# In the attention steps of a hybrid layer, all other TensorE work between QK and the product with V, and weight chunks made one ahead

## The chip, the cores and the metric

One core of a Trainium2 chip runs the whole kernel: one layer, 512 tokens, width 1024, all data in fp32. The metric is the device time of one execution in microseconds, lower is better; a kernel's time is the median of several runs. The engines are TensorE (PE; its weight loads are listed as PEld), VectorE (DVE), ScalarE (ACT), GpSimd (POOL) and SyncE (SP), which issues the DMAs here.

## The reference

```python
x = x + 0.5 * swiglu(rms_norm(x), w_gate1, w_up1, w_down1)
u = rms_norm(x) @ w_in          # -> c_q 384 | c_kv 256 | k_rope 32 | MoBA q, k, v 3 x 512
a = mla_attention(...)          # 8 heads, keys of 64 + 32 (rope), V of 64, causal
b = moba_attention(...)         # 8 heads of 64, blocks of 256 keys, top 3 past blocks + own, ALiBi
x = x + concat(a, b) @ w_out
x = x + 0.5 * swiglu(rms_norm(x), w_gate2, w_up2, w_down2)
return rms_norm(x)
```

`mla_attention` makes its queries and its keys and values from the low ranks (`q = rms_norm(c_q) @ w_uq`, `kv = rms_norm(c_kv) @ w_ukv`). With 512 tokens MoBA has two blocks, so every past block is chosen and both groups are causal softmax attention, MoBA's with a bias linear in the distance. The feed-forward width is 2816.

## The kernel before, in words

**Precision.** TensorE takes fp32 operands split in two parts, a high and a low one, and a product is three matmuls: high by high (L326), high by low (L327), low by high (L328), in `mm3`. Whatever feeds a matmul therefore passes ACT, which copies the high part, and DVE (or POOL), which subtracts it to get the low part. For weights these are L251 and L252 in `split`.

**Weights.** They come in chunks by DMA on SP's queue into raw slots. `pump(c, ahead)` makes chunks up to number c + ahead: it splits what has landed, frees the raw slot, and issues the DMA of a later chunk into it (`dma_fill`). The default of `ahead` is 2. For some chunks, those of the V projection, of the four pairs of MLA heads (ap0 to ap3) and of the first half of the output projection (wo0 to wo3), the low part is made by POOL, in two halves of 512 columns. `done(c)` gives the split slots back.

**Attention steps.** There are 16 steps, one per head: eight MoBA heads ("B"), then eight MLA heads ("A"). In step s the loop L1336 to L1344 writes:

- `pt(s-2)`: ten TensorE transposes (L1175) of the normalised scores P of head s-2 into three banks; ACT copies each bank's high part (L1178), DVE its low part (L1179).
- `qk(s)`: QK of head s into three banks (L1112 and L1113 for B, `mm3` for A); DVE adds mask or bias and takes the minimum (L1130, four), then frees the banks; ACT takes exp with row sums (L1138, four).
- `pv(s-2)`: eight matmuls of P by V (L1193) into one bank; ACT copies its lower half out (L1202), DVE adds the upper one (L1204) and frees the bank; each odd head also makes the two parts of the attention output (L1210 on ACT, L1211 on DVE).
- `normalise(s)`: DVE's reciprocal of the row sums (L1143), four multiplications on POOL (L1146), and four DMAs on SP's queue (L1149) that copy P to where `pt` reads it two steps later.
- `fillers(aim)`: pieces of other TensorE work from a queue, taken while half of the next piece still fits under `aim`.

**The fillers** (L1308 to L1325), with the cost in us that the queue writes for each: eight pieces of the MoBA projections of the last four heads, 12 matmuls each, 2.6 (`f_p`; at their end DVE L938, L941 and six half-height copies on ACT, L946, L948 and L949, with the low parts on DVE L947 and L950); four of the V projection, 6 matmuls, 1.3 (`f_uv`); for each pair of MLA heads one key piece, 6 matmuls, 1.3 (`f_uk`; ACT L1260, DVE L1261, and POOL L1262 for the shared rope rows) and two query pieces, 9 matmuls, 1.95 each (`f_uq`; DVE L1273, ACT L1277, DVE L1278); and eight pieces of the output projection's MoBA half, 12 matmuls, 2.6 (`f_wob`; DVE L1295 adds the bank to x). There are eight PSUM banks, handed out in the order in which they come free.

In each step the first call of `fillers` aims at 1.5 + 4.1 s, the second at that plus 3.2, so that some pieces come between QK and the product with V, and some behind `normalise`.

**The order on the engines.** What the program writes is recorded, and a scheduler then sets each engine's order by when it expects operands to be ready. Instructions of neighbouring parts can so change places.

Behind the steps come the remaining parts of the output projection (`wo_part`), which uses the last heads' transposes and products, and then the second feed-forward part, which is most of what follows 572 us.

Of the kernel before, what the change touches and what calls it, by code (L numbers as in the profile page):

```python
# [31 lines left out]
C0 = 128  # L32
OFF = (0, 128, 384, 768)
WARM = 9
LEAD, RATE, BACK = 1.5, 4.1, 3.2
SCRATCH = 1024

_P = 2.0 * math.pi
# [14 lines left out]
def layer_kernel(ctx, tc, xt, xtok, pos_row, pos_tok, gains, fin, consts, w, wc, out):  # L53
# [60 lines left out]
    def balloc():  # L114
        return bfree.popleft()
# [10 lines left out]
    def sput(s):  # L126
        (xfree if s < 8 else sfree if s < NR else efree).append(s)

    def sl(s):
        return ar[:, s, :] if s < NR else ext[s - NR][:, :]  # L130

    def slf(s):
        return sl(s).bitcast(F32)
# [6 lines left out]
    def hi_(s, rows=slice(0, 128)):  # L140
        return sl(s)[rows, 0:512]

    def lo_(s, rows=slice(0, 128)):
        return sl(s)[rows, 512:1024]
# [94 lines left out]
    def dma_fill():  # L239
        while state["dma"] < NCH and (ffree or fextra and state["dma"] in fourth):  # L240
            dma_chunk()
# [13 lines left out]
    def next_step(pieces=1):  # L255
        j = state["step"]
        kind = steps[j][0]
        state["step"] = j + 1
        if kind == "plain":
            c = steps[j][1]  # L260
            p = c in pooled
            hl[j] = split(fl(raw[c]), chunks[c][1], 2 if p else pieces, G if p else None)
            rfree(c)
            return
        if kind in PROD:
            b, q = steps[j][1]
            r = {i: b[i, q] for i in ("11", "12", "22", "21")}

            def add(o, i):
                V.tensor_tensor(fl(raw[r[o]]), fl(raw[r[o]]), fl(raw[r[i]]), op=OP.add)  # L270

            if kind == "q5":
                add("11", "12")
            elif kind == "p6":
                add("11", "22")
                add("12", "22")
            elif kind == "q4":
                add("21", "11")  # L280
                rfree(r["11"])
            i = {"q3": "22", "p7": "12", "p2": "21", "q4": "21"}.get(kind, "11")
            hl[j] = split(fl(raw[r[i]]), 1024)
            if kind in ("q3", "p7", "q4"):
                rfree(r[i])
            return
        _, (q11, q21, q22, q12) = steps[j]
        r = lambda c: fl(raw[c])
        if kind == 0:
            hl[j] = split(r(q11), 1024)  # L290
        elif kind == 1:
            V.tensor_tensor(sq, r(q21), r(q22), op=OP.add)
            hl[j] = split(sq, 1024)
        elif kind == 2:
            V.tensor_tensor(sq, sq, r(q11), op=OP.subtract)  # L295
            hl[j] = split(sq, 1024)
            V.tensor_tensor(r(q21), r(q11), r(q21), op=OP.subtract)  # L297
            rfree(q11)
        elif kind == 3:
            V.tensor_tensor(sq, r(q12), sq, op=OP.subtract)  # L300
            hl[j] = split(sq, 1024)
        else:
            c = (q21, q12, q22)[kind - 4]
            hl[j] = split(r(c), 1024)
            rfree(c)

    def room():
        return len(sfree) + (0 if state["lock"] else len(xfree))

    def pump(c, ahead=2):  # L310
        while state["step"] <= min(c + ahead, NST - 1) and (room() > 1 or state["step"] <= c):
            next_step()
            dma_fill()
# [11 lines left out]
    def mm3(ps, ah, al, bh, bl, start, stop, **kw):  # L325
        T.matmul(ps, lhsT=ah, rhs=bh, start=start, stop=False, **kw)  # L326
        T.matmul(ps, lhsT=ah, rhs=bl, start=False, stop=False, **kw)  # L327
        T.matmul(ps, lhsT=al, rhs=bh, start=False, stop=stop, **kw)  # L328
# [665 lines left out]
    for tp in range(2):  # L994
# [5 lines left out]
        for k in range(8):  # L1000
            c = c_c[k]
# [97 lines left out]
    def qk(s):  # L1099
        g, h = heads[s]  # L1100
        b1, b02, b3 = balloc(), balloc(), balloc()
        where = {0: (b02, 384), 1: (b1, 0), 2: (b02, 0), 3: (b3, 0)}
        for i in ORDER:
            b, o = where[i]
            n = 128 * (i + 1)
            p = banks[b][:, o:o + n]
            ts = slice(i * 128, i * 128 + 128)
            if g == "B":
                c = 512 * (h % 2)
                q = sl(QS["B", h // 2])[:, c + i * 128:c + i * 128 + 128]  # L1110
                kh, kl = KS["B", h // 2]
                T.matmul(p, lhsT=q, rhs=sl(kh)[:, c:c + n], start=True, stop=False)  # L1112
                T.matmul(p, lhsT=q, rhs=sl(kl)[:, c:c + n], start=False, stop=True)  # L1113
            else:
                q, k = QS["A", h], KS["A", h]
                mm3(p, hi_(q)[:, ts], lo_(q)[:, ts], hi_(k)[:, :n], lo_(k)[:, :n], True, True)
        if g == "A":
            sput(QS.pop(("A", h)))
            sput(KS.pop(("A", h)))
        elif h % 2:  # L1120
            sput(QS.pop(("B", h // 2)))
            for k in KS.pop(("B", h // 2)):
                sput(k)
        z = s % 2
        for i in ORDER:
            b, o = where[i]
            n = 128 * (i + 1)
            sc = 2.0 ** -(h + 1) if g == "B" else 1.0
            add = dist[:, OFF[i]:OFF[i] + n] if g == "B" else maskb[:, 512 - n:512]
            V.tensor_tensor_reduce(out=Sc[z][:, OFF[i]:OFF[i] + n], in0=banks[b][:, o:o + n],  # L1130
                                   in1=add, scale=sc, scalar=1e38, op0=OP.add, op1=OP.min,
                                   accum_out=mn[z][:, i:i + 1])
        for b in (b1, b02, b3):
            bfree.append(b)
        for i in ORDER:
            n = 128 * (i + 1)
            p = Sc[z][:, OFF[i]:OFF[i] + n]
            A.activation(p, p, AF.Exp, scale=-1.0, bias=mn[z][:, i:i + 1],  # L1138
                         accum_out=rs[z][:, i:i + 1])

    def normalise(s):
        z = s % 2
        V.reciprocal(ri[z], rs[z])  # L1143
        for i in range(4):
            p = Sc[z][:, OFF[i]:OFF[i] + 128 * (i + 1)]
            G.tensor_scalar(p, p, ri[z][:, i:i + 1], 1.0, op0=OP.mult, op1=OP.mult)  # L1146

            c, o = pcopy(s, i)
            nc.sync.dma_start(slf(c)[:, o:o + 128 * (i + 1)], p)  # L1149
# [4 lines left out]
    def pcopy(s, i):  # L1154
        if i == 1:
            return pq, 512 * (s % 2)
        if s not in PC:
            PC[s] = ealloc()
        return PC[s], {3: 0, 2: 512, 0: 896}[i]
# [3 lines left out]
    def pt(s):  # L1163
        z = s % 2
        PT[s] = {}
        for js in JB:
            b = balloc()
            o = 0
            slot = ealloc()
            for j in js:  # L1170
                PT[s][j] = (slot, o)
                for i in range(j, 4):
                    c, c0 = pcopy(s, i)
                    c0 += j * 128
                    T.transpose(banks[b][:, o:o + 128].bitcast(F32R), in_=sl(c)[:, c0:c0 + 128],  # L1175
                                identity=identr)
                    o += 128
            A.activation(hi_(slot)[:, :o], banks[b][:, :o], AF.Copy)  # L1178
            V.tensor_tensor(lo_(slot)[:, :o], banks[b][:, :o], hi_(slot)[:, :o].bitcast(F32),  # L1179
                            op=OP.subtract)  # L1180
            bfree.append(b)
        sput(PC.pop(s))
# [145 lines left out]
    def fillers(aim):  # L1328
        nonlocal spent
        while pieces and spent + pieces[0][0] / 2 < aim:  # L1330
            cost, c, f, args = pieces.popleft()
            pump(c)
            f(*args)
            spent += cost

    for s in range(16):  # L1336
        if s > 1:
            pt(s - 2)
        qk(s)
        fillers(LEAD + RATE * s)  # L1340
        if s > 1:
            pv(s - 2)
        normalise(s)
        fillers(LEAD + RATE * s + BACK if s < 15 else 1e9)  # L1344


    def wo_part(half, kks, accs, last=False):
# [29 lines left out]
    c = c_wo[6]  # L1377
# [5 lines left out]
    c = c_wo[7]  # L1383
# [163 lines left out]
```

## Time and profile before

| | |
|---|---|
| median of 3 runs | 935.31 us (934.46 to 935.58) |
| the profiled execution | 936.12 us, its span 934.3 us |
| mean granted TensorE clock | 0.998 |
| PE busy | 918.2 us, 98% |
| DVE, ACT, POOL busy | 751.7, 518.0, 138.7 us |
| attention steps | from about 424 to 572 us of the span |

A time in the profile counts from the span's start. A row of the timeline is: start, duration, engine, line, operation, output and inputs, shape, count; in brackets the engine's idle time ahead of it and what ended that. A row of the waits is: engine, output, line, then what released it, with total idle time, count and longest. In a group of instructions the numbers behind the first bar are the busy time and the mean in ns of one, behind the second the idle time before them. Matmuls are pipelined: the duration of one overlaps the next, so consecutive starts tell more than durations.

### The profile page before, as it was taken

The numbers are of one execution on the slowest core, as the hardware profiler recorded it, in microseconds if no ns is written. First come the engines' busy times: TensorE is split into PE (matmuls) and PEld (weight loads), VectorE is DVE, ScalarE is ACT, GpSimd is POOL, SyncE is SP. The second block draws the span as 40 slices with busy tenths as digits, with TensorE's granted clock in tenths as the row PEclk, the third lists the DMA queues.
The fourth block names the chain that finished last, engine by engine and source line by source line (L and its number), as shares of the span: only waits on it lengthen the run. The fifth ranks groups of instructions, "written<-read, shape, count | busy, mean of one in ns | idle before, by whom it ended". The sixth has DMA issues, their size and how long they took to land.

```text
span 934.3 us, 15098 instructions
## 1 busy us (share of the span) xinstructions
PE 918.2 (98%) x5901; PEld 835.8 (89%) x5901; DVE 751.7 (80%) x1091; ACT 518.0 (55%) x832; POOL 138.7 (15%) x172
## 2 busy tenths in 40 slices
PE   8999999999999999999999999999999999999997
PEld 6899999999888888988877788899999999988885
DVE  6999988899988844536789885989798879988845
ACT  7664545457355443627897864755555445735524
POOL 2059401000000000013676530000000000000001
PEclk9999999999999999999999999999999999999999
DMA  9423334236203515233433441123243223711302
GB/s 334 177 90 114 98 120 122 92 113 195 99 5 120 157 38 171 67 131 111 143 127 123 167 147 66 46 90 102 88 129 113 91 90 114 239 54 44 93 0 91
DMA packets 38088, 105.41 MB, mean 113 GB/s; under 512 B 4480, under 2 KB 11264, under 8 KB 38016
## 3 DMA queue, kind: packets, MB, share of 16 engines
q1 hardware_dynamic: 37008, 102.61, 33.6%
q10 hardware_dynamic: 1008, 1.84, 0.5%
q8 instruction: 46, 0.75, 0.3%
q14 instruction: 26, 0.21, 0.1%
HBM read 90.40 MB, written 2.10 MB: 99 GB/s over the span
## 4 chain that ended last, share of the span: by engine, by line
PE 44%; ACT 3%; DVE 2%; issue 2%; POOL 2%; DMA 0%; ACTq 0%; DVEq 0%; POOLq 0%
PE bank L485 22%; PE bank L326 7%; PE bank L327 7%; PE bank L328 7%; PE bank L1193 1%; ACT scr L1138 1%; POOL scr L1146 1%; PE bank L1175 1%; POOL ar L252 0%; ACT ar L251 0%; DVE ext L1179 0%; PE bank L402 0%; DMA ar<-scr 0%; ACT scr L1202 0%; DMA ext<-scr 0%
## 5 line engine op out<-in xcount | busy, mean ns | idle before, releaser
L485 PE MATMUL bank<-ar 128*128 128x256 f32 x3360 | 405.2, 283 | 2.0 <-DVE scr L516 0.8
L485 PEld LDWEIGHTS bank<-ar 128*128 128x128 f32 x3360 | 403.9, 192 | 3.1 <-DVE scr L516 1.3
L251 ACT ACTIVATE ar<-raw 128x1024 fp32r<-128x1024 f32 (+3 forms) x182 | 176.9, 982 | 148.2 <-issue 42.9
L326 PE MATMUL bank<-ar 128*128 128x512 f32 (+4 forms) x664 | 254.6, 384 | 2.5 <-ACT ar L251 1.3
L328 PE MATMUL bank<-ar 128*128 128x512 f32 (+4 forms) x664 | 253.2, 382 | 0.0
L327 PE MATMUL bank<-ar 128*128 128x512 f32 (+4 forms) x664 | 253.0, 381 | 0.1
L252 DVE TENSOR_TENSOR ar<-raw,ar 128x1024 fp32r<-128x1024 f32 (+2 forms) x164 | 192.3, 1182 | 54.3 <-ACT ar L251 35.5
L326 PEld LDWEIGHTS bank<-ar 128*128 128x128 f32 x664 | 124.6, 188 | 25.7 <-ACT ar L251 1.9
L328 PEld LDWEIGHTS bank<-ar 128*128 128x128 f32 x664 | 124.6, 188 | 23.2
L327 PEld LDWEIGHTS bank<-ar 128*128 128x128 f32 x664 | 124.8, 188 | 22.6 <-DVE ar L390 0.5
L251 ACT ACTIVATE ar<-sq 128x1024 fp32r<-128x1024 f32 x62 | 65.7, 1059 | 86.0 <-DVE sq L295 27.0
L252 DVE TENSOR_TENSOR ar<-sq,ar 128x1024 fp32r<-128x1024 f32 x62 | 75.8, 1223 | 10.2 <-ACT ar L251 10.1
L1412 POOL TENSOR_TENSOR x<-x,tabs 128x512 f32<-128x512 f32 x4 | 5.2, 1289 | 353.6 <-ACT scr L354 353.6
L1146 POOL TENSOR_SCALAR scr<-scr,sm 128x128 f32<-128x128 f32 (+1 forms) x64 | 41.2, 664 | 42.4 <-DVE sm L1143 41.6
L617 DVE SCALAR_TENSOR_TENSOR x<-bank,sm,x 128x512 f32<-128x512 f32 x37 | 27.0, 745 | 23.9 <-PE bank L328 23.9
L1138 ACT ACTIVATE scr<-scr,sm 128x256 f32<-128x256 f32 (+1 forms) x64 | 35.3, 553 | 17.9 <-DVE sm L1130 17.9
L495 ACT ACTIVATE scr<-bank 128x512 f32<-128x512 f32 x60 | 34.9, 581 | 6.3 <-PE bank L485 6.3
L354 ACT ACTIVATE scr<-x 128x512 f32<-128x512 f32 x28 | 17.6, 631 | 29.2 <-DVE x L617 27.0
L575 ACT ACTIVATE ar<-h 128x512 fp32r<-128x512 f32 x28 | 17.2, 630 | 17.0 <-PE bank L327 8.8
L252 POOL TENSOR_TENSOR ar<-raw,ar 128x512 fp32r<-128x512 f32 x18 | 23.5, 1320 | 9.2 <-ACT ar L251 8.3
L295 DVE TENSOR_TENSOR sq<-sq,raw 128x1024 f32<-128x1024 f32 x20 | 24.4, 1222 | 0.5
L297 DVE TENSOR_TENSOR raw<-raw,raw 128x1024 f32<-128x1024 f32 x20 | 24.5, 1225 | 0.2
(239 smaller groups left out, 930.2 us busy)
## 6 DMA issues: line engine op xcount, KB each, us to landing
raw<-in_w_dram SPq DMA_DIRECT2D x144, 512.0 KB, 3.5
h<-in_w_dram SPq DMA_DIRECT2D x8, 512.0 KB, 3.8
ext<-scr SPq DMA_DIRECT2D x13, 256.0 KB, 2.4
raw<-in_wc_dram SPq DMA_DIRECT2D x8, 336.0 KB, 3.1
ext<-scr SPq DMA_DIRECT2D x13, 192.0 KB, 2.2
x<-in_xtok_dram SPq DMA_DIRECT2D x4, 512.0 KB, 8.2
ext<-scr SPq DMA_DIRECT2D x16, 128.0 KB, 2.1
xs<-in_xt_dram SPq DMA_DIRECT2D x5, 256.0 KB, 5.2
```

The source lines that it names most:

```text
L251: A.activation(sl(h)[:, a:b], src[:, a:b], AF.Copy)
L252: (e or V).tensor_tensor(sl(l)[:, a:b], src[:, a:b], slf(h)[:, a:b], op=OP.subtract)
L295: V.tensor_tensor(sq, sq, r(q11), op=OP.subtract)
L297: V.tensor_tensor(r(q21), r(q11), r(q21), op=OP.subtract)
L326: T.matmul(ps, lhsT=ah, rhs=bh, start=start, stop=False, **kw)
L327: T.matmul(ps, lhsT=ah, rhs=bl, start=False, stop=False, **kw)
L328: T.matmul(ps, lhsT=al, rhs=bh, start=False, stop=stop, **kw)
L485: T.matmul(o, lhsT=a_[:, ws], rhs=b_[:, xs_], start=first and e == 0 and k == 0 and n == 0, stop=k == 3 and n == 2, skip_group_check=True)
L495: A.activation(t, banks[b], AF.Copy)
L617: V.scalar_tensor_tensor(xs, banks[b], r, xs, op0=OP.mult, op1=OP.add)
L1138: A.activation(p, p, AF.Exp, scale=-1.0, bias=mn[z][:, i:i + 1], accum_out=rs[z][:, i:i + 1])
L1146: G.tensor_scalar(p, p, ri[z][:, i:i + 1], 1.0, op0=OP.mult, op1=OP.mult)
```

## The change

`LEAD` goes from 1.5 to 4.7 and `BACK` (3.2) goes away. 1.5 + 3.2 is 4.7, so a step's aim at its end is what it was. The loop calls `normalise(s)` directly behind `qk(s)`, then all the step's fillers, then the product with V; the last step takes what is left behind it. Within the steps `pump` makes one chunk ahead instead of two.

```diff
-LEAD, RATE, BACK = 1.5, 4.1, 3.2
+LEAD, RATE = 4.7, 4.1
...
-            pump(c)
+            pump(c, 1)
...
         if s > 1:
             pt(s - 2)
         qk(s)
+        normalise(s)
         fillers(LEAD + RATE * s)
         if s > 1:
             pv(s - 2)
-        normalise(s)
-        fillers(LEAD + RATE * s + BACK if s < 15 else 1e9)
+        if s == 15:
+            fillers(1e9)
```

The pieces per step stay the same ones, up to one piece of the last steps. TensorE in step 5, from the end of QK of head 5 to the product of head 3 (L1193), before; the `mm3` into bank4 and bank1 are V-projection pieces:

```order
L1113 MATMUL bank5_86<-ar_61 128x512
L326 MATMUL bank4_85<-ar_61 128x512
L327 MATMUL bank4_85<-ar_61 128x512
L328 MATMUL bank4_85<-ar_61 128x512
L326 MATMUL bank4_85<-ar_61 128x512
L327 MATMUL bank4_85<-ar_61 128x512
L328 MATMUL bank4_85<-ar_61 128x512
L1193 MATMUL bank7_88<-ext5_3129,ext6_3130 128x512 x2
L326 MATMUL bank1_82<-ar_61 128x512
L327 MATMUL bank1_82<-ar_61 128x512
L1193 MATMUL bank7_88<-ar_61,ext7_3131 128x384
```

The same place after, from the last matmul of the first piece on; the transposes (L1175) are already those of head 4, and bank5 is the one that the product of head 2 held:

```order
L328 MATMUL bank4_85<-ar_61 128x512
L1175 MATMUL bank7_88<-identr_76,ext10_3134 128x128
L1175 MATMUL bank7_88<-identr_76,ext1_3125 128x128
L1175 MATMUL bank3_84<-identr_76,ext1_3125 128x128
L326 MATMUL bank5_86<-ar_61 128x512
L327 MATMUL bank5_86<-ar_61 128x512
L328 MATMUL bank5_86<-ar_61 128x512
L326 MATMUL bank5_86<-ar_61 128x512
L327 MATMUL bank5_86<-ar_61 128x512
L328 MATMUL bank5_86<-ar_61 128x512
L326 MATMUL bank1_82<-ar_61 128x512
L327 MATMUL bank1_82<-ar_61 128x512
```

Four more matmuls into bank1 and then the product of head 3 follow. Before, six matmuls stood between QK and the product, now 18 and three transposes.

POOL around the normalisation (L1146) of heads 10 and 11, before; L252 from raw1 is the second chunk of the output projection, wo1, and the L1146 are those of heads 9 and 10:

```order
L1146 TENSOR_SCALAR scr_74<-scr_74,sm_78 128x512
L252 TENSOR_TENSOR ar_61<-raw1_63,ar_61 128x512 x2
L1262 TENSOR_SCALAR ar_61<-ar_61 64x1024
L1262 TENSOR_SCALAR ext3_3127<-ar_61 64x1024
L1146 TENSOR_SCALAR scr_74<-scr_74,sm_78 128x128
L1146 TENSOR_SCALAR scr_74<-scr_74,sm_78 128x256
L1146 TENSOR_SCALAR scr_74<-scr_74,sm_78 128x384
L1146 TENSOR_SCALAR scr_74<-scr_74,sm_78 128x512
```

After, where the first L1146 is the last of head 10 and the next four are those of head 11:

```order
L1146 TENSOR_SCALAR scr_74<-scr_74,sm_78 128x512
L252 TENSOR_TENSOR ar_61<-raw1_63,ar_61 128x512
L1146 TENSOR_SCALAR scr_74<-scr_74,sm_78 128x128
L1146 TENSOR_SCALAR scr_74<-scr_74,sm_78 128x256
L1146 TENSOR_SCALAR scr_74<-scr_74,sm_78 128x384
L1146 TENSOR_SCALAR scr_74<-scr_74,sm_78 128x512
L252 TENSOR_TENSOR ar_61<-raw1_63,ar_61 128x512
```

Both halves of wo1 stood ahead of head 10's normalisation; now the second half stands behind head 11's.

DVE in step 11, behind the last mask instruction (L1130) of head 11, before; L252 is a weight chunk's low part, L1143 the reciprocal:

```order
L1273 SCALAR_TENSOR_TENSOR scr_74<-bank7_88,tabs_73 128x512
L252 TENSOR_TENSOR ar_61<-raw0_62,ar_61 128x1024
L1278 TENSOR_TENSOR ext5_3129<-scr_74,ext5_3129 128x512
L1204 TENSOR_TENSOR scr_74<-bank1_82,scr_74 64x512
L1143 RECIPROCAL sm_78<-sm_78 128x4
L1295 TENSOR_TENSOR x0_69<-bank2_83,x0_69 128x512
L1211 TENSOR_TENSOR ar_61<-scr_74,ar_61 128x512
```

After:

```order
L1273 SCALAR_TENSOR_TENSOR scr_74<-bank5_86,tabs_73 128x512
L252 TENSOR_TENSOR ar_61<-raw5_67,ar_61 128x1024
L1143 RECIPROCAL sm_78<-sm_78 128x4
L1278 TENSOR_TENSOR ext0_3124<-scr_74,ext0_3124 128x512
L252 TENSOR_TENSOR ar_61<-raw0_62,ar_61 128x1024
L1295 TENSOR_TENSOR x0_69<-bank1_82,x0_69 128x512
L1204 TENSOR_TENSOR scr_74<-bank2_83,scr_74 64x512
```

The reciprocal stood behind L1278 and the evacuation of the product (L1204); now it stands ahead of both, and L1204 behind L1295.

## The prediction

> **What bounds the kernel now.** I read the page's busy shares first, then the stretch of the attention steps by itself, then what TensorE waits for in it, then the places one by one in the timeline.
>
> ```profile
> PE 918.2 (98%) x5901; PEld 835.8 (89%) x5901; DVE 751.7 (80%) x1091; ACT 518.0 (55%) x832; POOL 138.7 (15%) x172
> ```
>
> TensorE is busy for 918.2 of 934.3 us. The change neither adds nor removes a matmul, so all that it can give is time in which TensorE stands, and only in the steps that it reorders. Two windows divide these from what follows (start and end, length, then busy time of PE, PEld, DVE, ACT and POOL, then granted clock):
>
> ```profile
> 424.00:572.00 148.00, 144.06 (x814) 121.10 (x813) 120.89 (x283) 114.41 (x267) 75.07 (x94) 1.00 0.40 136
> 572.00:926.00 354.00, 354.00 (x2376) 328.48 (x2375) 289.11 (x348) 180.15 (x242) 5.16 (x4) 1.00 0.27 87
> ```
>
> Behind 572 us TensorE never stands, so what is won ahead of it is won at the end, one for one, and what is lost there too. In the steps it is busy 144.06 of 148.00. DVE (120.89) and ACT (114.41) are not full, so this is a matter of which wait ends when. The waits of PE in that window name their causes (total, count, longest):
>
> ```profile
> PE bank L326 <- DVE ar L1261: 1.4, 2, 1.0
> PE bank L1193 <- ACT ar L1178: 1.0, 1, 1.0
> PE bank L1193 <- DVE ext L1179: 0.8, 3, 0.3
> PE bank L1193 <- DVE ar L1261: 0.4, 1, 0.4
> PEld bank L1175 <- DMA ar<-scr: 0.4, 2, 0.2
> PEld bank L1112 <- DVE scr L1204: 0.4, 1, 0.4
> ```
>
> These understate the loss, since a modelled end of a matmul reaches into the wait that follows. The better measure is start to start, less what the columns take. Columns are priced from the longest run without a wait, the 12 matmuls of one piece of the output projection:
>
> ```profile
> 520.87 0.62 PE L1193 MATMUL bank<-ext,ext 128*128 128x512 f32 x2
> 522.10 0.45 PE L326 MATMUL bank<-ar 128*128 128x512 f32 x1
> 524.89 0.96 PE L1175 MATMUL bank<-identr,ext 128*128 128x128 f32 x10
> ```
>
> From 522.10 to 524.89 are 12 matmuls of 512 columns, 0.233 us each; the eight of a product with V take 522.10 - 520.87 = 1.23 us. By this measure, the product with V that waits longest:
>
> ```profile
> 467.09 0.40 PE L327 MATMUL bank<-ar 128*128 128x512 f32 x1
> 468.51 0.45 PE L1193 MATMUL bank<-ar,ext 128*128 128x384 f32 x1 [1.02 <-ACT ar L1178]
> ```
>
> 468.51 - 467.09 is 1.42, less 0.23: 1.19 lost, and 0.11 behind it. Done for every place of the window that loses over 0.1 us (followers of 0.11 counted with it), the products with V lose 0.61 (at 450.0), 1.30 (468.5), 0.11 (476.4), 0.68 (484.1), 0.27 (502.3), 0.50 (512.2), 0.66 (528.4) and 0.11 (565.5): **4.24**. Two matmuls that wait for a bank lose more, both behind L1261:
>
> ```profile
> 501.56 0.50 PE L326 MATMUL bank<-ar 128*128 128x512 f32 x1 [0.41 <-DVE ar L1261]
> 516.64 0.34 PE L328 MATMUL bank<-ext,ar 128*128 128x384 f32 x1
> 518.01 0.50 PE L326 MATMUL bank<-ext,ar 128*128 128x512 f32 x1 [1.03 <-DVE ar L1261]
> 518.58 0.39 PE L328 MATMUL bank<-ext,ar 128*128 128x512 f32 x1
> ```
>
> The second is 1.37 from 516.64, less 0.17 for 384 columns: 1.20, with its follower 1.31; the first 0.79 by the same count; together **2.10**. The first transposes behind the DMA of P lose **0.63**, a QK that waits for the bank of L1204 **0.38** (the PEld rows above). In all 7.35 us: the change cannot give more than that, and 0.2% of the time, about what a measurement of this kernel can tell from no change, is 1.87.
>
> **The change, part by part.**
>
> *Fillers ahead of V.* Before, steps 3, 7, 9, 12, 13 and 15 had hardly a matmul between QK and the product with V; after, each step has at least 12, that is 12 x 0.233 = 2.8 us more for the transposes' halves (L1178, L1179) to be made. The largest of these waits was 1.30, so I take all eight away: **-4.24**. That holds where the half was late by its own work. The 1.30 was not: ACT had six copies ahead of L1178.
>
> ```profile
> 464.08 1.29 ACT L946 ACTIVATE ext<-scr 64x512 fp32r<-64x512 f32 x2
> 467.35 0.63 ACT L949 ACTIVATE ext<-scr 64x512 fp32r<-64x512 f32 x1
> 467.88 0.84 ACT L1178 ACTIVATE ar<-bank 128x512 fp32r<-128x512 f32 x2
> 463.31 0.73 DVE L938 SCALAR_TENSOR_TENSOR scr<-bank,cst,rB 128x512 f32<-128x512 f32 x1
> ```
>
> *What is late next there.* The copies run from 464.08 to 467.98, 3.9 us. In the new order the whole projection of that step ends just ahead of step 4's V, so what stands behind the copies is no longer L1178 but the evacuation of that product (L1202, L1204), whose bank the second V-projection piece of step 5 takes. Their prices and the work that runs on TensorE meanwhile:
>
> ```profile
> L1204 DVE TENSOR_TENSOR scr<-bank,scr 64x512 f32<-64x512 f32 x16 | 10.9, 684 | 7.2 <-ACT scr L1202 7.2
> L1202 ACT ACTIVATE scr<-bank 64x512 f32<-64x512 f32 x16 | 9.5, 597 | 3.1 <-PE bank L1193 2.8
> 471.73 0.97 PE L1175 MATMUL bank<-identr,ext 128*128 128x128 f32 x10
> 472.54 0.35 PE L1112 MATMUL bank<-ext,ext 128*128 128x256 f32 x1
> 473.88 0.39 PE L326 MATMUL bank<-ar 128*128 128x512 f32 x1
> ```
>
> Chain: 0.73 + 3.9 + 0.60 + 0.68 = 5.9. TensorE: product 1.23, transposes 0.81 (471.73 to 472.54), QK 1.34 (to 473.88), six matmuls 1.40, three early transposes 0.24: 5.0. A new wait of 0.9, or 1.3 if it is as long as the one it replaces; I take **+1.1**.
>
> *Banks behind L1261.* Two such waits stay possible (the query piece of step 8, the third bank of QK 11), at other places. Nothing in the trace shows them in the new order: none at the least, twice 1.31 at the most; I take the middle, 1.3, against 2.10 before: **-0.8**.
>
> *Chunks one ahead.* Before, POOL split the second chunk of the output projection (wo1), both halves, at
>
> ```profile
> 508.73 2.54 POOL L252 TENSOR_TENSOR ar<-raw,ar 128x512 fp32r<-128x512 f32 x2
> ```
>
> and the piece that first uses it began at 522.10, 13 us later. The splits are the same in number; each comes one piece group later, and with it the weight load that takes its raw slot on SP's queue. With such a lead a chunk later is hidden in most places. Not here: wo1 now takes slots that the last query pieces of steps 10 and 11 still read, and POOL's order becomes first half, normalise of head 11, second half. The last two matmuls of step 11's piece (L327, L328) wait for that second half. The rows:
>
> ```profile
> 518.60 0.68 DVE L1278 TENSOR_TENSOR ext<-scr,ext 128x512 fp32r<-128x512 f32 x1
> 521.16 0.68 DVE L1130 CUSTOM_DVE_ANT_0 scr<-bank,cst 128x512 f32<-128x512 f32 x1
> 522.37 1.21 DVE L252 TENSOR_TENSOR ar<-raw,ar 128x1024 fp32r<-128x1024 f32 x1
> 537.79 0.40 PE L328 MATMUL bank<-ar,ext 128*128 128x512 f32 x1
> 538.90 0.69 DVE L1130 CUSTOM_DVE_ANT_0 scr<-bank,cst 128x512 f32<-128x512 f32 x1
> L1273 DVE SCALAR_TENSOR_TENSOR scr<-bank,tabs 128x512 f32<-128x512 f32 x8 | 5.4, 680 | 0.7 <-PE bank L328 0.7
> L1143 DVE RECIPROCAL sm<-sm 128x4 f32<-128x4 f32 x16 | 2.8, 176 | 7.8 <-ACT scr L1138 7.8
> 488.36 3.30 POOL L1146 TENSOR_SCALAR scr<-scr,sm 128x128 f32<-128x128 f32 x4
> 515.20 2.07 POOL L1146 TENSOR_SCALAR scr<-scr,sm 128x128 f32<-128x128 f32 x4 [1.45 <-DVE sm L1143]
> 519.81 1.29 POOL L252 TENSOR_TENSOR ar<-raw,ar 128x512 fp32r<-128x512 f32 x1 [2.54 <-ACT ar L251]
> ```
>
> From the end of a QK to the end of its L1130: 1.57 (538.90 + 0.69 less 537.79 + 0.23) to 3.03 (521.16 + 0.68 less 518.58 + 0.23). Then on DVE L1273 0.68, a split 1.21, the reciprocal 0.18; on POOL the four L1146, 2.07 to 3.30, and the half, 1.29. Sum 7.0 to 9.7. TensorE has meanwhile 18 matmuls (4.2), the product with V, one matmul and three transposes (1.23 + 0.23 + 0.24): 5.9. A new wait of 1.1 to 3.8; middle **+2.5**.
>
> *Normalise ahead of the fillers.* DVE's reciprocal now stands ahead of L1278, L1295 and L1204, and these wait with it for exp's sums. L1204 is wanted only for a bank some pieces on, and P not until two steps later (its four DMAs on SP's queue go out earlier), so nothing. If that cover is gone, it costs what the L1143 row shows, 7.8 / 8 = 1.0 at a place.
>
> *Sum.* Kept 0.63 and 0.38; new 1.1, 1.3, 2.5, and 0.11 behind each of the three, 0.3: 6.2 against 7.35, **-1.2**. The profiled execution took 936.12 us, 1.8 beyond its span, so its own forecast is 934.9; it lies 0.8 above the median of 935.31, and from the median it is **934.1**.
>
> [...]
>
> ```profile
> 510.00 1.82 DVE L1278 TENSOR_TENSOR ext<-scr,ext 128x512 fp32r<-128x512 f32 x1
> ```
>
> L1278 takes 0.68 alone (at 518.60) and 1.82 beside POOL's split of 508.73. [...]
>
> **The rivals.**
>
> R1, the new order covers all: wo1's half is in time (L1130 early as at 538.90, L1146 2.07, and the scheduler finds other matmuls ahead), and L1261's banks are free. Left are 0.63, 0.38, the 1.1 and one bank wait of 0.5: 2.6, that is -4.8: **930.5**. For it: the products of steps 4, 8, 11, 13 and 14 lose nothing even before. Against it: the row of 521.16.
>
> R2, slower, one mechanism: POOL's row at step 11. If the first half of wo1 starts only when the reciprocal is done, it stands in the chain too: 9.7 + 1.3 - 5.9 = 5.1, and with L1261's banks held as long as before (DVE being as late as at 521.16), 0.63 + 0.38 + 1.1 + 2.1 + 5.1 + 0.3 = 9.6, +2.3: **937.6**. The whole is slower than before once that place loses over 7.35 - (0.63 + 0.38 + 1.1 + 2.1 + 0.3) = 2.8 us, and by over 0.2% from 4.7. For it: ACT's L251 came late in before too (POOL waited 2.54 for it at 519.81). Against it: in POOL's new row the first half stands ahead of head 11's L1146.
>
> R3, POOL and DVE stretch each other at step 11: the four L1146 take 3.30, not the middle 2.69, wait 3.1: **934.8**. [...]
>
> R4, the change does less than it says: the scheduler had already drawn matmuls forward (at 467.09 a filler stands just ahead of V), and each wait returns at another place: **935.3**.
>
> **How the numbers follow.** The forecast has 0.45, its own range 932.0 to 936.0 from the ends of the three estimates taken not all at once; 0.13 of that lies more than 0.2% below the median (under 933.4). R1 has 0.23, R2 0.13, R3 0.11, R4 0.08. Faster 0.13 + 0.23 = 0.36; slower 0.13; same the rest, 0.51. The range goes into R1 and up to R2: 930.8 to 937.0 leaves out about 0.1 at either end.
>
> **What would show it.** Right: no wait of over 0.2 us at L1193 in the steps; a wait of about 1 us at a V-projection matmul of step 5 behind L1204; one of 1 to 4 at L327 of step 11 behind POOL's L252; nothing lost behind the steps. Wrong: a V product still behind L1179, the step-11 wait absent (R1) or over 3.8 (R2), or a new wait in a step that I took as covered.

## The result: 1.1% slower, and the profile after

The changed kernel takes 945.29 us (median of 4 runs, 944.19 to 946.66) against 935.14 us before: a ratio of 1.0107, interval 1.0095 to 1.0119. The forecast was 934.1 in a range of 930.8 to 937.0; the rival that was slower stood at 937.6. The time lies beyond both.

The profiled execution took 946.66 us, its span is 944.8. From the first matmul of QK of head 0 to the last of the last product with V, TensorE took 144.8 us before and 154.9 after (10.1 more); behind that it took 356.0 us in both. So the loss lies where it was looked for, in the attention steps, and what follows was not touched. What was not expected is in two lines of the page after, TensorE's busy time and its granted clock in the 40 slices:

```profile
PE 924.1 (98%) x5901; PEld 843.3 (89%) x5901; DVE 753.0 (80%) x1091; ACT 517.1 (55%) x832; POOL 141.2 (15%) x172
PEclk9999999999999999999999799999999999999999
```

The same 5901 matmuls are busy for 5.9 us longer than before (918.2), and one slice has a clock of 7 tenths where before all had 9. Finer windows of after (the clock is the last but two of the columns) show where:

```profile
424.00:582.00 158.00, 148.91 (x814) 127.10 (x813) 121.54 (x282) 113.14 (x267) 77.16 (x94) 0.96 0.37 126
494.64:498.05 3.41, 3.41 (x10) 2.67 (x9) 2.80 (x11) 3.11 (x10) 1.28 (x1) 0.50 0.34 135
521.95:525.36 3.41, 3.41 (x9) 2.67 (x8) 2.44 (x10) 1.89 (x6) 0.92 (x1) 0.50 0.56 204
532.19:539.02 6.83, 6.57 (x24) 5.79 (x25) 5.24 (x14) 3.18 (x9) 0.21 (x1) 0.50 0.51 196
```

TensorE ran at half its clock for three stretches of 3.41, 3.41 and 6.83 us, each beside the end of a wait: the first two begin 1.3 and 0.8 us behind it (494.64 and 521.95, the waits end at 493.35 and 521.15), the third 0.3 us ahead of it (532.19, 532.46). In the timeline of after a matmul of 512 columns then takes 0.43 us from start to start, not 0.23:

```profile
495.01 0.63 PE L326 MATMUL bank<-ar 128*128 128x512 f32 x1
495.44 0.63 PE L327 MATMUL bank<-ar 128*128 128x512 f32 x1
```

Counted matmul by matmul (start to start, less the columns at full clock, in these stretches alone, without the waits in them) that is 1.4 + 1.6 + 2.9 = **5.9 us**. The other 10.1 - 5.9 = **4.2** are waits. The list of PE's waits in the steps, after:

```profile
PE bank L327 <- POOL ar L252: 3.2, 2, 2.9
PE bank L1175 <- DMA ext<-scr: 2.2, 2, 1.2
PE bank L326 <- DVE ext L1261: 1.6, 1, 1.6
PE bank L326 <- DVE ar L1261: 0.9, 1, 0.9
PE bank L326 <- DVE scr L1204: 0.7, 1, 0.7
PE bank L1112 <- DVE scr L1204: 0.3, 1, 0.3
```

No product with V (L1193) waits any more: eight waits of 4.24 us are gone, as the change meant them to be. In their place stand fewer and longer ones. Start to start they are these.

*Step 5, 2.55 us.* The scheduler put three transposes of head 4 ahead of the second V-projection piece, and P of head 4 was not there. PE, POOL, ACT and DVE of after:

```profile
466.24 0.39 PE L328 MATMUL bank<-ar 128*128 128x512 f32 x1
467.61 0.25 PE L1175 MATMUL bank<-identr,ext 128*128 128x128 f32 x1 [0.99 <-DMA ext<-scr]
469.07 0.37 PE L1175 MATMUL bank<-identr,ext 128*128 128x128 f32 x2 [1.20 <-DMA ext<-scr]
463.67 3.97 POOL L1146 TENSOR_SCALAR scr<-scr,sm 128x128 f32<-128x128 f32 x4 [0.94 <-DVE sm L1143]
466.98 0.59 ACT L1202 ACTIVATE scr<-bank 64x512 f32<-64x512 f32 x1
467.81 0.68 DVE L1204 TENSOR_TENSOR scr<-bank,scr 64x512 f32<-64x512 f32 x1
```

Head 4's four multiplications took 3.97 us on POOL, beside DVE's L947 and L950, which read two SBUF tiles each; four such took 2.07 at 515.20 of before, where the DVE instructions beside them (L1261, L1204, L1273) read a PSUM bank and one tile. No run shows whether the DVE instructions beside them made the difference. The bank that the forecast spoke of, of head 2's product, comes free at 468.5 (L1204's end), hidden behind the transposes. The matmul of 466.24 was through its columns at 466.5, so without the transposes that bank alone would have made TensorE wait for 2.0 us: the transposes add 0.5.

*Banks behind the evacuations of key pieces, 2.2 us in step 8 and 1.9 at QK of head 11.*

```profile
490.81 0.40 PE L328 MATMUL bank<-ar 128*128 128x512 f32 x1
491.90 0.51 PE L326 MATMUL bank<-ar 128*128 128x512 f32 x1 [0.69 <-DVE scr L1204]
493.35 0.51 PE L326 MATMUL bank<-ar 128*128 128x512 f32 x1 [0.94 <-DVE ar L1261]
519.21 0.34 PE L328 MATMUL bank<-ar 128*128 128x384 f32 x1
521.15 0.50 PE L326 MATMUL bank<-ar 128*128 128x512 f32 x1 [1.61 <-DVE ext L1261]
517.42 0.57 ACT L1260 ACTIVATE ext<-bank 64x512 fp32r<-64x512 f32 x1
519.56 0.58 ACT L1260 ACTIVATE ext<-bank 64x512 fp32r<-64x512 f32 x1
520.41 0.69 DVE L1261 TENSOR_TENSOR ext<-bank,ext 64x512 fp32r<-64x512 f32 x1
```

ACT copies the first half of a key piece (L1260) behind the step's exp, the second only at 519.56, behind three other copies; DVE's L1261 follows at 520.41, and QK at 521.15. The first of the two waits of step 8 is one behind L1204, the evacuation of a product.

*Second half of wo1 in step 11, 3.1 us.*

```profile
521.73 0.43 PE L328 MATMUL bank<-ar 128*128 128x512 f32 x1
529.13 0.43 PE L1175 MATMUL bank<-identr,ext 128*128 128x128 f32 x3
532.46 0.79 PE L327 MATMUL bank<-ar 128*128 128x512 f32 x1 [2.90 <-POOL ar L252]
525.80 0.69 DVE L1273 SCALAR_TENSOR_TENSOR scr<-bank,tabs 128x512 f32<-128x512 f32 x1 [1.41 <-PE bank L328]
527.54 0.17 DVE L1143 RECIPROCAL sm<-sm 128x4 f32<-128x4 f32 x1
521.59 1.28 POOL L252 TENSOR_TENSOR ar<-raw,ar 128x512 fp32r<-128x512 f32 x1
527.81 3.36 POOL L1146 TENSOR_SCALAR scr<-scr,sm 128x128 f32<-128x128 f32 x4 [4.94 <-DVE sm L1143]
531.15 1.25 POOL L252 TENSOR_TENSOR ar<-raw,ar 128x512 fp32r<-128x512 f32 x1
```

From the reciprocal on this is the chain of the forecast: normalisation of head 11, second half, matmul. Both of its sums came out longer, though. From the end of QK 11 (521.73 + 0.23) to the end of the half (531.15 + 1.25) are 10.4 us, where 7.0 to 9.7 were forecast, because L1273 waited 1.41 for a query piece that TensorE did at half clock; TensorE's own work from there to the transposes at 529.13 took 7.4, not 5.9, for the same reason. The difference, 3.1, fell into the range.

Besides, 0.6 us stay at the first transposes, 0.6 at a QK, and 0.8 are new behind the half of another chunk at 557. Sum 11.8 against 7.35, 4.4 more, which fits the 4.2.

### The profile page after: what moved, and what is told of

It reads as the page before. It is cut to its first block, busy times and chain, and to the rows that moved or that the text cites. A ratio compares the mean times of both kernels' runs of the same rounds, so it can differ in the third digit from the quotient of the medians.

```text
span 944.8 us, 15116 instructions
## 1 busy us (share of the span) xinstructions
PE 924.1 (98%) x5901; PEld 843.3 (89%) x5901; DVE 753.0 (80%) x1091; ACT 517.1 (55%) x832; POOL 141.2 (15%) x172
## 4 chain that ended last, share of the span: by engine, by line
PE 86%; DVE 5%; issue 4%; POOL 3%; ACT 1%; DMA 1%; ACTq 0%; SPq 0%; DVEq 0%; POOLq 0%
PE bank L485 40%; PE bank L327 14%; PE bank L328 14%; PE bank L326 14%; POOL scr L1146 2%; PE bank L1193 1%; POOL ar L252 1%; DVE ar L252 1%; PE bank L1175 1%; PE bank L402 1%; DMA gn<-in_gains_dram 0%; DVE raw L297 0%; POOL xs L727 0%; PE bank L1112 0%; DVE h L469 0%
## 5 line engine op out<-in xcount | busy, mean ns | idle before, releaser
L485 PEld LDWEIGHTS bank<-ar 128*128 128x128 f32 x3360 | 403.8, 192 | 3.2 <-DVE scr L516 1.4
L326 PE MATMUL bank<-ar 128*128 128x512 f32 (+3 forms) x676 | 260.8, 386 | 4.8 <-DVE ext L1261 1.6
L327 PE MATMUL bank<-ar 128*128 128x512 f32 (+3 forms) x676 | 259.8, 385 | 3.2 <-POOL ar L252 3.2
L328 PE MATMUL bank<-ar 128*128 128x512 f32 (+3 forms) x676 | 259.3, 384 | 0.0
L252 DVE TENSOR_TENSOR ar<-raw,ar 128x1024 fp32r<-128x1024 f32 (+2 forms) x164 | 192.9, 1185 | 57.5 <-ACT ar L251 50.8
L326 PEld LDWEIGHTS bank<-ar 128*128 128x128 f32 x676 | 128.4, 190 | 29.4 <-ACT ar L251 2.2
L327 PEld LDWEIGHTS bank<-ar 128*128 128x128 f32 x676 | 128.5, 190 | 27.1 <-POOL ar L252 4.2
L328 PEld LDWEIGHTS bank<-ar 128*128 128x128 f32 x676 | 128.5, 190 | 23.7
L252 DVE TENSOR_TENSOR ar<-sq,ar 128x1024 fp32r<-128x1024 f32 x62 | 75.9, 1224 | 10.2 <-ACT ar L251 10.1
L1146 POOL TENSOR_SCALAR scr<-scr,sm 128x128 f32<-128x128 f32 (+1 forms) x64 | 43.1, 691 | 55.2 <-DVE sm L1143 42.3
L1179 DVE TENSOR_TENSOR ext<-bank,ext 128x512 fp32r<-128x512 f32 (+1 forms) x46 | 25.7, 601 | 0.3
L252 POOL TENSOR_TENSOR ar<-raw,ar 128x512 fp32r<-128x512 f32 x18 | 23.5, 1312 | 8.8 <-ACT ar L251 7.5
```

Of the source, the lines that this page charges most:

```text
L252: (e or V).tensor_tensor(sl(l)[:, a:b], src[:, a:b], slf(h)[:, a:b], op=OP.subtract)
L485: T.matmul(o, lhsT=a_[:, ws], rhs=b_[:, xs_], start=first and e == 0 and k == 0 and n == 0, stop=k == 3 and n == 2, skip_group_check=True)
```

## The experiments

All were compared with runs of the kernel before on the same chip. "Steps" is TensorE's time from the first QK to the last product, of the profiled execution; "half" the time at half clock in it.

| kernel | median us | ratio to before | steps us | half us |
|---|---|---|---|---|
| before | 935.1 to 935.7 | | 144.8 | 0 |
| after | 945.29 | 1.0107 (1.0095 to 1.0119) | 154.9 | 13.7 |
| wo1's low part on DVE | 939.18 | 1.0036 (1.0024 to 1.0049) | 147.5 | 3.4 |
| 12 matmuls in the wait | 943.45 | 1.0084 (1.0070 to 1.0098) | 149.6 | 0 |
| 12 matmuls, no wait | 941.36 | 1.0057 (1.0044 to 1.0071) | 149.9 | 3.4 |
| order alone | 942.11 | 1.0072 (1.0053 to 1.0092) | 149.8 | 6.8 |
| one ahead alone | 940.58 | 1.0051 (1.0036 to 1.0067) | 148.7 | 0 |
| after, normalise behind V | 949.11 | 1.0142 (1.0125 to 1.0160) | 157.6 | 17.1 |
| before, normalise early | 936.47 | 1.0005 (0.9996 to 1.0014) | 144.4 | 0 |
| wo1 and head 4 on DVE | 940.10 | 1.0049 (1.0035 to 1.0063) | 147.6 | 3.4 |
| order in six steps | 936.05 | 1.0006 (0.9997 to 1.0015) | 144.4 | 0 |
| order alone, query first | 940.60 | 1.0055 (1.0041 to 1.0069) | 149.7 | 10.2 |
| before, query first | 936.55 | 1.0005 (0.9996 to 1.0014) | 144.8 | 0 |
| six steps, query first | 942.39 | 1.0062 (1.0049 to 1.0074) | 150.8 | 10.2 |

**Is the half clock set off by the waits?** The first run takes the longest wait away, in the new kernel:

```diff
-    pooled = {steps[j][1] for j in [c_uv, *c_ap, *c_wo[:4]]}
+    pooled = {steps[j][1] for j in [c_uv, *c_ap, c_wo[0], *c_wo[2:4]]}
```

> The new kernel, with the low part of wo1 made by DVE instead of POOL (in one piece of 1024, not two of 512). Theory A: the step-11 wait of 3.1 us goes, and with it the two windows of 3.41 us at half clock that follow it, which cost 3.4: 945.3 - 6.5 = 938.8, range 937.5 to 940.5. If slow windows are not set off by waits: 945.3 - 3.1 = 942.2, with as much time at half clock as before the edit.

Measured 939.18, 6.1 less than after, though only 3.1 of waiting were removed. Its windows show full clock where after had half (530 to 540), and one stretch of half clock, behind step 5, where after had none:

```profile
470.24:473.65 3.41, 3.41 (x10) 2.74 (x10) 2.08 (x5) 2.29 (x8) 0.56 (x1) 0.50 0.08 29
530.00:540.00 10.00, 10.00 (x55) 8.42 (x53) 8.54 (x20) 5.69 (x15) 3.75 (x6) 1.00 0.60 202
```

Not all of the 6.1 comes from the removed wait and its stretch. The waits of step 8 and of QK 11 are still there, nearly as long as in after (0.9 and 1.6), and are no longer followed by half clock (0.99 is the clock of its steps, what the one stretch makes it):

```profile
PE bank L326 <- DVE ext L1261: 1.4, 1, 1.4
PE bank L326 <- DVE ar L1261: 1.0, 1, 1.0
```

In the profiled executions the steps are 7.4 us shorter: 3.1 of waiting, 2.9 of the stretch behind it, and the rest because half clock now follows one of the other waits and not two. So this run alone does not show that the stretch hung on the wait that was removed; the next two bear on it more directly.

The second run leaves the cause of the wait and takes the idling: TensorE gets work in it.

```diff
+            if half == 0 and t == 0 and kk == 3:
+                d = balloc()
+                for _ in range(12):
+                    T.matmul(banks[d], lhsT=hi_(attnT[7])[:, 0:128], rhs=whi(c1)[:, 512:1024],
+                             start=True, stop=True)
+                bfree.append(d)
             wo_mm((c0, c1)[kk // 2], kk % 2, 4 + kk, t, b, kk == 0, kk == 3)
```

> The new kernel with 12 more matmuls (2.8 us of columns), whose results nobody reads, in TensorE's order just ahead of the one that waited 3.1 us for wo1's second half in step 11. They run while it would wait. If the slow windows are set off by TensorE's idling (theory A): the wait shrinks below 0.5 us, the windows of half clock at 532 to 539 go, and 2.8 us more of work make the kernel faster by up to 3.4: 941.5 to 943.5. If slow windows have another cause, or come with the work: 945 (hidden, nothing else moves) to 948.

The control has the same 12 matmuls in the kernel with wo1's low part on DVE, where TensorE does not wait there:

> Control for the run with 12 more matmuls: the same 12 in the kernel with wo1's low part on DVE (939.2), where nothing waits at that place. Theory A: they cost their columns, 12 x 0.233 = 2.8 us: 941 to 943. If 12 more matmuls help TensorE by themselves (as they did where it waited): 939 or less.

With the wait, 12 more matmuls made the kernel 1.8 us faster (943.45 against 945.29); without it, 2.2 slower (941.36 against 939.18). By the ratios to before on the same chip it is 2.2 faster and 2.0 slower, each uncertain by about 1.7. The place in the timeline of the first:

```profile
528.87 0.39 PE L326 MATMUL bank<-ar 128*128 128x512 f32 x1
530.04 0.50 PE L327 MATMUL bank<-ar 128*128 128x512 f32 x1 [0.79 <-POOL ar L252]
```

and the window of its steps, at full clock throughout in this execution:

```profile
424.00:578.00 154.00, 147.01 (x831) 125.54 (x831) 122.44 (x283) 114.00 (x268) 76.62 (x94) 1.00 0.39 130
```

The wait did not shrink below 0.5 as expected, but to 0.9, and the gain is at the lower end of what was expected. With 2.2 us less of waiting and 2.8 more of work, waits alone would have made the kernel 0.6 slower. The profiled execution is the fastest of the four (941.79, mean clock 0.998); the others took 942.69 to 944.37 at 0.994 to 0.996, so they probably had half clock elsewhere, which no trace shows. In the profile the waits of step 5, step 8 and QK 11 were there (2.2, 0.7 + 1.0 and 1.6 us in its list of waits), and no half clock followed, which leads to the next point.

**Which wait sets it off.** Length alone does not tell. In after step 5's 2.55 us were followed by full clock (1.00 from 466 to 490), the 2.2 of step 8 and the 1.9 at QK 11 by half. The starts of its half-clock stretches are 27.31 and 10.24 us apart, 8 and 3 times 3.41. Let its steps be divided into pieces of 3.41 us that begin and end there, and let TensorE stand in the time from start to start that the columns do not take. Then it stood for 2.0 us from 491.23 to 494.64, 2.0 from 518.54 to 521.95 and 2.9 from 528.78 to 532.19, and half clock follows each of the three. The next fullest piece has 1.8 us (467.34 to 470.75; the division parts step 5's 2.55), and full clock follows. Divided in the same way from the half clock at its end (929.93), before has at most 1.3 us in a piece, and a clock of 1.00 in all its steps. In the other runs, too, the same wait went with either clock: the transposes of step 5 waited for 2.2 us by the lists of the kernel with wo1 on DVE and of that with the 12 matmuls, and half clock followed at 470.24 in the first and nowhere in the second. That the place of a wait in such a division decides is the author's reading of the traces of after and before, and so is the 2.0 us in the expectations of two of the last runs, below; neither was shown for the other runs. Why the stretch of after at 532 lasted for 6.83 us, though TensorE stood for only 0.7 us of its first half, is not settled.

**Which part of the change makes the waits.** The order alone, with chunks two ahead and normalise behind the product (the diff is against after):

```diff
-            pump(c, 1)
+            pump(c)
...
         qk(s)
-        normalise(s)
         fillers(LEAD + RATE * s)
         if s > 1:
             pv(s - 2)
+        normalise(s)
```

> The order of the fillers alone: all between QK and the product with V, chunks two ahead as before, normalise behind the product as before. Theory A: no wait for wo1; the waits of step 5's early transposes (2.5 us) and behind L1261 (about 4) stay with one or two slow windows (1.7 each): 936 to 941. Theory B (chunks one ahead are the whole cause): 933 to 936. Theory C (the order is the cause): 944 to 946.

942.11, a little beyond theory A's range. Its profile has 2.2 us more waiting than before (149.8 - 144.8 = 5.0, less 2.8 for 6.8 us at half clock, counted as above). The longest wait reads

```profile
520.20 0.40 PE L326 MATMUL bank<-ar 128*128 128x512 f32 x1
523.27 0.79 PE L326 MATMUL bank<-ext,ar 128*128 128x512 f32 x1 [2.68 <-DVE ext L1261]
```

and step 5's transposes wait for 3.3 us. Behind the wait of the row, matmuls of 512 columns start 0.42 us apart (523.87 to 524.29). The chunks one ahead alone, in the old loop (`pump(c, 1)`, nothing else):

> The old loop (fillers on both sides of the product with V, normalise behind it), with chunks one ahead as the only edit. Theory A (TensorE loses 3.4 us more to waits and 6.8 us to windows at half clock that these waits set off; the waits come from the order of the fillers together with the late second half of wo1): POOL's row has both halves of wo1 between heads 10 and 11 here, so they come late by 1 us at most: 935 to 938 us, no window at half clock in the steps. Theory B (chunks one ahead are the whole cause): 944 to 946. Theory C (the fillers' order alone is the cause): 935.

940.58: theory A's range missed by 2.6 us. Its waits are many and short, 3.8 us more in the steps than before, and the clock stays full there:

```profile
424.00:575.00 151.00, 143.86 (x809) 120.02 (x808) 122.18 (x282) 114.16 (x267) 75.56 (x94) 1.00 0.40 133
```

The longest of its waits in all, by cause:

```profile
PE bank L327 <- POOL ar L252: 1.7, 3, 0.8
PE bank L1112 <- DVE scr L1204: 1.3, 1, 1.3
```

So neither part is the whole cause: alone they cost 7.0 and 5.4 us, and with normalise early, as in after, together 10.1. The order pays more in clock than in waits, the chunks pay in waits alone. Of their 5.4 the steps of the profiled execution show 3.8; it was 1.0 us longer ahead of the steps too, as were executions with chunks two ahead (that of normalise early in the old loop, for one), so this is not put down to the chunks. Normalise's place, in the new loop and in the old:

```diff
         qk(s)
-        normalise(s)
         fillers(LEAD + RATE * s)
         if s > 1:
             pv(s - 2)
+        normalise(s)
```

> The new loop, with normalise put back behind the product with V. Theory A: POOL still has head 11's normalisation between the two halves of wo1, so the step-11 wait stays (2 to 3 us and its slow windows); if the early reciprocal holds up L1261 and L1204 on DVE, the two bank waits go: 939 to 943. If normalise's place in the loop does nothing (the scheduler places it): 944 to 946. Theories B and C both: 944 to 946.

> The kernel before, with normalise written directly behind QK as the only edit. TensorE's order stays that of the kernel before up to a few matmuls in the last step. Theory A (order of the fillers and lateness of the chunks make the waits, normalise's place does not): 935 to 936.5, no window at half clock in the steps. If the early reciprocal holds up DVE: 938 or more.

The first of these two is also the order and the chunks together without the third edit: 14.0 us over before, more than 7.0 + 5.4. Put back behind the product in the new loop, normalise costs 3.8 us more than in after (949.11), which no theory had: QK 11 waits for 4.8 us there,

```profile
526.88 0.79 PE L326 MATMUL bank<-ext,ar 128*128 128x512 f32 x1 [4.59 <-DVE ext L1261]
```

and in the old loop, early, it changes nothing that can be told (936.47 against 935.53). The early reciprocal is not the fault; in the new loop it saves time.

**Can it be mended?** With wo1 on DVE, head 4's multiplications were put there too, so that the scheduler leaves its transposes behind the product:

```diff
-            G.tensor_scalar(p, p, ri[z][:, i:i + 1], 1.0, op0=OP.mult, op1=OP.mult)
+            (V if s == 4 else G).tensor_scalar(p, p, ri[z][:, i:i + 1], 1.0, op0=OP.mult,
+                                               op1=OP.mult)
```

> The new kernel with wo1's low part on DVE (the earlier run, 939.2) and, besides, the four multiplications of head 4's normalise on DVE instead of POOL. The scheduler then leaves head 4's transposes behind the product of step 5. Theory A: the wait of 2.5 us for the DMA of head 4's P in step 5 goes and the slow window behind it (1.7), but a V-projection piece waits about 1.1 us for the bank of head 2's product, as was forecast: 939.2 - 2.5 - 1.7 + 1.1 = 936.1, range 935 to 938. If the wait only moves: 939.

940.10, missed: the transposes no longer wait, but the V-projection piece does, for the bank of head 2's product (L1204 stands one line lower here):

```profile
466.52 0.40 PE L328 MATMUL bank<-ar 128*128 128x512 f32 x1
470.49 0.79 PE L326 MATMUL bank<-ar 128*128 128x512 f32 x1 [3.57 <-DVE scr L1205]
```

It is the wait that the forecast put here, at 3.7 us, not 1.1, since DVE now has the multiplications, and the low parts behind them, ahead of L1205: it starts at 469.75, though ACT's copy was done at 467.9. The other trials move fillers in six steps of the old loop only, or change the order of two pieces (in the order alone, in the kernel before, and in the six steps):

```diff
-        fillers(LEAD + RATE * s)
+        fillers(LEAD + RATE * s + (BACK if s in (3, 7, 9, 12, 13, 15) else 0))
```

> The kernel before, with the fillers moved ahead of the product with V in steps 3, 7, 9, 12, 13 and 15 only, where hardly a matmul stood there; chunks two ahead, normalise behind. Theory A: the products' waits in these steps go (0.6 + 0.7 + 0.3 + 0.7 + 0.1 = 2.4 us), nothing long enough for a slow window comes: 932.7 to 935. If each wait returns elsewhere: 935.1; if one of over 1.8 us comes with a slow window: 937 or more.

```diff
-        pieces.append((1.3, c_ap[j], f_uk, (j,)))
         pieces.append((1.95, c_ap[j], f_uq, (j, 0)))
+        pieces.append((1.3, c_ap[j], f_uk, (j,)))
```

> The order alone with chunks two ahead (the earlier run, 942.1), and in each pair of MLA heads the first query piece ahead of the key piece, whose bank is freed latest (two copies on ACT, then two subtractions on DVE, L1261). Theory A: the wait of 2.85 us of QK 11 behind L1261 goes with its slow window (1.7): 937 to 939. If the bank wait comes from the place ahead of the product with V and not from the kind of piece: 941 to 943.

> The kernel before, with each pair's first query piece ahead of its key piece as the only edit. Theory A: the two bank waits behind L1261 (0.79 and 1.31 us) go or shrink, no window has 2 us of idle TensorE: 933 to 935. If the bank waits move to other pieces: 935.5 to 936.5.

> The fillers ahead of the product with V in six steps, and the first query piece ahead of the key piece. Theory A: as the run of the six steps (936.05), less the bank waits of 0.72 and 1.32 us behind L1261, no slow window: 933.5 to 936. If waits fall together in one window of 3.41 us with 2.0 us or more of idle TensorE, 1.7 is added: 937 to 938.

Six steps: 936.05, no change, missed by 1. Query first: 940.60, missed; the waits behind L1261 shrink, but transposes now wait for a P,

```profile
508.96 0.28 PE L1175 MATMUL bank<-identr,ar 128*128 128x128 f32 x1 [1.65 <-DMA ar<-scr]
```

with half clock behind it (from 510.29 on 384 columns take 0.31 us, not 0.17). Query first in the old order: 936.55, no change, missed by 1.5, with no half clock in the steps. Both: 942.39, missed, 10.2 us at half clock. None of these versions beats the kernel before.

## Why the prediction was wrong

Right: what bounds the kernel; that the products' eight waits go (-4.24); that nothing moves behind the steps; that step 11 would wait for wo1's second half behind head 11's normalisation (forecast 2.5 of 1.1 to 3.8, measured 3.1, with L1146 at 3.36, just over its long end); that normalise's place costs nothing. That the 3.1 lies inside its range is in part luck: the chain took 10.4, beyond its longest, 9.7, and the work that covers it 7.4, not 5.9.

Wrong in size, by its terms:
- *Step 5*, forecast 1.1, measured 2.55. The three early transposes stood in the order rows, and were counted as cover of 0.24 us; that they need head 4's P nearly a step early, behind an L1146 that took 3.97, was not asked. The bank wait lay hidden behind them, and was itself larger, 2.0 where 1.1 was forecast: the chain from the product's start (461.7) to L1204's end took 6.8, not 5.9, as mask instructions (L1130) stood ahead of L938 and of L1204 on DVE and exp ahead of the copies on ACT, and without the transposes TensorE covered 4.8 of it.
- *Banks behind L1261*, forecast 1.3 with 2.6 as the upper end, measured 2.2 + 1.9 (0.9 of it behind L1204). "Twice 1.31 at the most" was a guess from the row of another order; ACT's row, with exp ahead of L1260, might have priced it.
- *Chunks one ahead* were worked through at one place. 0.8 us came at another (557), and by themselves they cost 5.4. The places that were taken as hidden were not: the prediction's own sign of being wrong, a new wait in a step that counted as covered.

These make +4.4 where -1.2 was forecast: 939.5, outside the range already.

Wrong in kind: the sentence that what is lost in the steps "is lost there too" one for one. Each wait was priced by its length. Three of the waits, alone or with a neighbour, made TensorE stand for 2.0, 2.0 and 2.9 of the 3.41 us ahead of a stretch at half clock, and these stretches cost 1.4 to 2.9 us more each, 5.9 in all. That standing sets it off rests on these three, on the 12 matmuls that made the kernel 1.8 us faster where it waited and 2.2 slower where it did not, and, less cleanly, on the run that removed a wait of 3.1 and gained 6.1. The prediction put this term at nothing. No row of before could show it in the steps, since its waits there reach 1.3 us and its clock is 1.00. R2 had the right sign and the right place, but not the mechanism: POOL made the first half of wo1 at 521.59, ahead of the reciprocal, and then stood idle for 4.94 us. What came at step 11 is R3's, the four L1146 at 3.36 and a wait of 3.1; its 934.8 missed by the other waits and by the clock.

## What to carry to other kernels

Removing many short waits of TensorE at the price of a few long ones can lose more than their sum tells (here 4.2 us more of waits cost 10.1): besides the total, look at how much standing falls close together (in after 2.0, 2.0 and 2.9 us of 3.41 stood ahead of the half clock). When an order puts work together ahead of the last consumer, follow what then comes due at once (banks, slots, transposed operands), each through its own engine's row. And ask of every instruction that a scheduler moved forward whether its operand is there, by measured times.

## What was not expected of the hardware

In the steps of after TensorE's clock fell to half for 3.41, 3.41 and 6.83 us. In the piece of 3.41 us ahead of each it had stood for 2.0, 2.0 and 2.9 us; behind a piece with 1.8 us the clock stayed full. The same kernel ran at different mean clocks: six runs of the kernel with wo1's low part on DVE took 937.80 us at a mean clock of 0.998, 938.73 to 940.21 at 0.996 to 0.997, and 940.31 at 0.993; only the one of 940.21 was traced, so where the others lost clock is not shown. Idle TensorE time can be worth filling with work that nobody reads, if the wait cannot be removed: the filling gained 1.8 us here, removing the wait 6.1.
